# im2col on one core: the first load in two parts ahead of the barrier, single-plane copies, a first store in halves

## The chip, the core and the metric

The kernel runs on one of the cores of a Trainium2 chip. It uses three kinds of workers of that core: the DMA engines (16 of them), which move data between device memory (DRAM) and the core's on-chip memory; VectorE (DVE in the profile) and ScalarE (ACT), which copy inside the on-chip memory; and SyncE (SP), which issues the transfers. The on-chip memory has 128 partitions; a tile "128x900" has 900 numbers in each of them. TensorE (PE) and GpSimd (POOL) have no part in the computation.

The metric is the device time of one execution in microseconds (us).

## The reference

For an input of 16 images with 64 channels of 32x32 floats, `im2col` with a 3x3 kernel writes, for each image and channel, nine planes of 30x30: plane (ki, kj) is the channel's image, shifted by ki rows and kj columns.

```
for b in range(batch):
    for i in range(h_out):          # 30
        for j in range(w_out):      # 30
            patch = x[b, :, i:i+3, j:j+3]
            cols[b, :, i*w_out + j] = patch.ravel()
# cols: (16, 64*9, 900) float32
```

No arithmetic is done. 4.19 MB are read and 33.18 MB are written, nine planes of 900 for each channel of 1024.

## The kernel before

The 16x64 channels lie on 128 partitions, eight channels (`CPP`) on each. One input tile holds all eight channels, 32 KB per partition. It is loaded in two parts by SP: the first two channels (rows 0 to 64 of the 256 rows of 32 floats, 8 KB per partition) and the other six (24 KB per partition). Line 35 issues both.

The loop runs over four pairs of channels. For a pair there is an output tile of 2 x 9 x 900 floats (64.8 KB per partition); the pool has two buffers of it, so the third pair's copies wait until the first pair's store has landed. For each channel ScalarE copies the three planes of ki = 1 in one instruction (L55, 128x2700). VectorE copies the first two planes of ki = 0 and of ki = 2, two per instruction (L57, 128x1800). The planes that are left, (0,2) and (2,2), are one VectorE instruction for the first channel of a pair (L61), and one of VectorE (L65) and one of ScalarE (L68) for the second. Then SP stores the pair with one transfer of 64.8 KB per partition (L71), which in DRAM is contiguous for each partition.

The schedule is written by hand: each engine does its instructions in the order of the program, and waits at an instruction until the semaphores that it names have been reached. The order of transfers on SP's queue is the order in which they are issued. An instruction that must wait for several semaphores has the further ones in event instructions ahead of it. ScalarE's first copy brings a load of its function table (ACT_TABLE_LOAD, shown under L55), which is put directly ahead of that copy. After the program is compiled, the first load is taken out of its place and put at the very start, ahead of SP's drain, which begins the opening barrier of all engines; the rest of the work begins behind that barrier.

Of the kernel before, what the change touches and what calls it, by code (L numbers as in the profile page):

```python
# [1 line left out]

# [3 lines left out]


def _im2col(ctx, tc, x, K, out):


    nc = tc.nc
    P = nc.NUM_PARTITIONS

    B, C, H, W = x.shape
    HO = H - K + 1
    WO = W - K + 1
    KK = K * K
    assert out.shape == (B, C * KK, HO * WO)
    CPP = B * C // P
    assert CPP * P == B * C and C % CPP == 0 and CPP % 2 == 0 and K == 3  # L20

    x_v = x.rearrange("b (cp c2) h w -> (b cp) (c2 h w)", c2=CPP)
    out_v = out.rearrange("b (cp c2 kk) n -> (b cp) c2 (kk n)", c2=CPP, kk=KK)

    in_pool = ctx.enter_context(tc.tile_pool(name="in_pool", bufs=1))
    out_pool = ctx.enter_context(tc.tile_pool(name="out_pool", bufs=2))

    ctx.enter_context(tc.manual_schedule())

    in_tile = in_pool.tile([P, CPP, H, W], x.dtype, name="in_tile")  # L30
    in_flat = in_tile.rearrange("p c h w -> p (c h w)")

    def load(r0, r1):

        return nc.sync.dma_start(
            out=in_flat[:, r0 * W : r1 * W],
            in_=x_v[:, r0 * W : r1 * W],
        )

    first = load(0, 2 * H)  # L40
    load(2 * H, CPP * H)

    def planes(c, ki, kj, n, step):

        w = in_tile[:, c, ki : ki + HO, kj : kj + WO]
        part, row, col = [list(d) for d in w.ap]
        return bass.AP(w.tensor, w.offset, [part, [step, n], row, col])

    for c in range(0, CPP, 2):
        out_tile = out_pool.tile([P, 2, KK, HO, WO], x.dtype, name="out_tile")  # L50


        for s in range(2):
            o = out_tile[:, s]
            nc.scalar.copy(out=o[:, K : 2 * K], in_=planes(c + s, 1, 0, K, 1))  # L55
            for ki in (0, 2):
                nc.vector.tensor_copy(  # L57
                    out=o[:, ki * K : ki * K + 2], in_=planes(c + s, ki, 0, 2, 1)
                )
            if s == 0:  # L60
                nc.vector.tensor_copy(  # L61
                    out=o[:, 2:KK:6], in_=planes(c + s, 0, 2, 2, 2 * W)
                )
            else:
                nc.vector.tensor_copy(  # L65
                    out=o[:, 2], in_=in_tile[:, c + s, 0:HO, 2 : 2 + WO]
                )
                nc.scalar.copy(  # L68
                    out=o[:, 8], in_=in_tile[:, c + s, 2 : 2 + HO, 2 : 2 + WO]
                )  # L70
        nc.sync.dma_start(  # L71
            out=out_v[:, c : c + 2].rearrange("p c n -> p (c n)"),
            in_=out_tile.rearrange("p c kk i j -> p (c kk i j)"),
        )
    return first


def kernel(
    tc: tile.TileContext,
    x: bass.AP,  # L80
    kernel_size: bass.AP,
    out: bass.AP,
):
    with ExitStack() as ctx:
        first = _im2col(ctx, tc, x, int(kernel_size), out)


    tc.close()
    tc.compile()  # L89
    blocks = tc.nc.main_func.blocks  # L90
    load = first.ins
    home = next(b for b in blocks if any(i.name == load.name for i in b.instructions))
    home.instructions = [i for i in home.instructions if i.name != load.name]
    head = list(blocks[0].instructions)
    at = next(
        k
        for k, i in enumerate(head)
        if i.engine == load.engine and type(i).__name__ == "InstDrain"
    )
    head.insert(at, load)  # L100
    blocks[0].instructions = head


# [1 line left out]
_INS = ['x', 'kernel_size']  # L105
_OUTS = [((16, 576, 900), 'float32')]

_NUMBERS = {'kernel_size': 3}


# [26 lines left out]
```

## Time and profile before

| what | value |
|---|---|
| median of 3 runs | 91.33 us (91.1 to 91.39) |
| profiled execution | 91.39 us, of which 89.6 are the span |
| VectorE busy | 22.6 us, 24 instructions |
| ScalarE busy | 23.8 us, 13 instructions |
| DMA queue | 864 packets, 37.37 MB, 97.2% of 16 engines' span |
| copy on ScalarE, 128x2700 / 128x900 | 2443 / 938 ns |
| copy on VectorE, 128x1800 / 128x900 | 1092 / 620 ns |
| table load on ScalarE | 1283 ns, once |

The span goes from the first instruction of the program to the last; the time of a run has about 1.8 us more around it. In the profile "SPq" is SP issuing a transfer; a transfer's landing is when its semaphore is reached. A line of the timeline gives the start and the duration in us, the engine, the line of the kernel, the operation and the shape; in brackets stands how long the engine had been idle before, and what ended that. Instructions of one kind that follow one another are merged into one line ("x2"). Where two copies follow directly, the second starts a little before the first one's end.

### The profile page before, as it was taken

How to read it: one execution, taken by the hardware profiler on the slowest of the kernel's cores; microseconds unless marked ns; L12 is line 12 of the kernel's file. 1: busy time of each engine (PE TensorE's matmuls, PEld its weight loads, DVE VectorE, ACT ScalarE, POOL GpSimd, SP SyncE). 2: the span in 40 equal slices, each digit the busy share in tenths (PEclk: the TensorE clock that was granted, in tenths of full speed). 3: DMA queues.
4: the chain of work that ended last, by engine and by line, in shares of the span. 5: the costliest groups of instructions: out<-in, count | busy, mean ns of one | idle time of the engine just before them, and what ended most of it. 6: DMA issues, size and time to landing. Idle time of an engine off the chain costs nothing.

```text
span 89.6 us, 96 instructions
## 1 busy us (share of the span) xinstructions
DVE 22.6 (25%) x24; ACT 23.8 (27%) x13; POOL 0.2 (0%) x4
## 2 busy tenths in 40 slices
DVE  0079759900000099500000399100000000000000
ACT  5079759900000099500000399100000000000000
POOL 0000000000000000000000000000000000000000
DMA  5989899999999999947999999999999982999990
GB/s 128 505 384 494 362 463 463 463 463 463 463 463 463 463 463 463 434 174 318 463 463 463 463 463 463 463 463 463 463 463 463 463 347 116 463 463 463 463 463 0
DMA packets 864, 37.37 MB, mean 417 GB/s; under 512 B 96, under 2 KB 96, under 8 KB 96
## 3 DMA queue, kind: packets, MB, share of 16 engines
q1 hardware_dynamic: 864, 37.37, 97.2%
HBM read 4.19 MB, written 33.18 MB: 417 GB/s over the span
## 4 chain that ended last, share of the span: by engine, by line
DMA 49%; DVE 12%; DVEq 1%; issue 0%; SPq 0%
DMA out_dram<-out_tile 36%; DMA in_tile<-in_x_dram 13%; DVE out_tile L57 8%; DVE out_tile L61 2%; DVE out_tile L65 1%; DVEq L89 1%; DVEq L57 0%; SPq L71 0%
## 5 line engine op out<-in xcount | busy, mean ns | idle before, releaser
L55 ACT COPY out_tile<-in_tile 128x2700 f32<-128x2700 f32 x8 | 19.2, 2443 | 31.7 <-DMA out_dram<-out_tile 27.1
L57 DVE COPY out_tile<-in_tile 128x1800 f32<-128x1800 f32 x16 | 16.8, 1092 | 33.7 <-DMA out_dram<-out_tile 27.1
L61 DVE COPY out_tile<-in_tile 128x1800 f32<-128x1800 f32 x4 | 4.4, 1090 | 0.0
L68 ACT COPY out_tile<-in_tile 128x900 f32<-128x900 f32 x4 | 3.8, 938 | 0.0
L65 DVE COPY out_tile<-in_tile 128x900 f32<-128x900 f32 x4 | 2.5, 620 | 0.0
L55 ACT ACT_TABLE_LOAD x1 | 1.3, 1283 | 0.8 <-PEq L118 0.8
L118 POOL MEMSET const-bfloat16-1.0<- 128x1 bf16 x1 | 0.1, 101 | 0.0
L118 POOL MEMSET const-uint8-127<- 128x1 uint8 x1 | 0.1, 101 | 0.0
L118 POOL MEMSET const-float32-0.0<- 128x1 f32 x1 | 0.1, 98 | 0.2 <-issue 0.2
L118 POOL MEMSET const-float32-1.0<- 128x1 f32 x1 | 0.1, 98 | 0.0
## 6 DMA issues: line engine op xcount, KB each, us to landing
out_dram<-out_tile SPq DMA_DIRECT2D x4, 8100.0 KB, 32.4
in_tile<-in_x_dram SPq DMA_DIRECT2D x1, 3072.0 KB, 11.4
in_tile<-in_x_dram SPq DMA_DIRECT2D x1, 1024.0 KB, 4.9
```

The lines of the kernel that those rows point to most:

```text
L55: nc.scalar.copy(out=o[:, K : 2 * K], in_=planes(c + s, 1, 0, K, 1))
L57: nc.vector.tensor_copy(out=o[:, ki * K : ki * K + 2], in_=planes(c + s, ki, 0, 2, 1))
L61: nc.vector.tensor_copy(out=o[:, 2:KK:6], in_=planes(c + s, 0, 2, 2, 2 * W))
L65: nc.vector.tensor_copy(out=o[:, 2], in_=in_tile[:, c + s, 0:HO, 2 : 2 + WO])
L68: nc.scalar.copy(out=o[:, 8], in_=in_tile[:, c + s, 2 : 2 + HO, 2 : 2 + WO])
L89: tc.compile()
L118: nc = _bacc.Bacc("TRN2", target_bir_lowering=False, num_devices=1)
```

## The change

The first load is now two: rows 0 to 16 (2 KB per partition) and rows 16 to 64 (6 KB). Both are put at the very start, ahead of SP's drain. The third part, 24 KB, is issued where the second one was.

Each plane is a copy of its own (128x900), 72 in all. For channel 0, ScalarE takes the six planes with kj = 0 or 2 and VectorE the three with kj = 1. From then on a pattern of five gives two planes to ScalarE and three to VectorE. The first pair is stored in two transfers, one for each channel (32.4 KB per partition), each issued when its nine planes are there; the other three pairs are stored as before.

```diff
-    first = load(0, 2 * H)
-    load(2 * H, CPP * H)
+    cuts = [0, 16, 2 * H, CPP * H]
+    first = [load(nc.sync, r0, r1) for r0, r1 in zip(cuts[:2], cuts[1:3])]
+    load(nc.sync, cuts[2], cuts[3])
...
+    on_act = (False, True, False, True, False)
+    n = 0
     for c in range(0, CPP, 2):
         out_tile = out_pool.tile([P, 2, KK, HO, WO], x.dtype, name="out_tile")
         for s in range(2):
-            o = out_tile[:, s]
-            nc.scalar.copy(out=o[:, K : 2 * K], in_=planes(c + s, 1, 0, K, 1))
-            for ki in (0, 2):
-                nc.vector.tensor_copy(
-                    out=o[:, ki * K : ki * K + 2], in_=planes(c + s, ki, 0, 2, 1)
-                )
-            if s == 0:
-                nc.vector.tensor_copy(
-                    out=o[:, 2:KK:6], in_=planes(c + s, 0, 2, 2, 2 * W)
+            for kk in range(KK):
+                ki, kj = divmod(kk, K)
+                src = in_tile[:, c + s, ki : ki + HO, kj : kj + WO]
+                dst = out_tile[:, s, kk]
+                if kk % 3 != 1 if c + s == 0 else on_act[n % len(on_act)]:
+                    nc.scalar.copy(out=dst, in_=src)
+                else:
+                    nc.vector.tensor_copy(out=dst, in_=src)
+                n += 1
+            if c == 0:
+                nc.sync.dma_start(
+                    out=out_v[:, s],
+                    in_=out_tile[:, s].rearrange("p kk i j -> p (kk i j)"),
                 )
-            else:
-                nc.vector.tensor_copy(
-                    out=o[:, 2], in_=in_tile[:, c + s, 0:HO, 2 : 2 + WO]
-                )
-                nc.scalar.copy(
-                    out=o[:, 8], in_=in_tile[:, c + s, 2 : 2 + HO, 2 : 2 + WO]
-                )
-        nc.sync.dma_start(
-            out=out_v[:, c : c + 2].rearrange("p c n -> p (c n)"),
-            in_=out_tile.rearrange("p c kk i j -> p (c kk i j)"),
-        )
+        if c > 0:
+            nc.sync.dma_start(
+                out=out_v[:, c : c + 2].rearrange("p c n -> p (c n)"),
+                in_=out_tile.rearrange("p c kk i j -> p (c kk i j)"),
+            )
     return first
...
-    load = first.ins
...
+    for load in (f.ins for f in first):
...
+        head.insert(at, load)
+        blocks[0].instructions = head
```

More of the change, by code (lines that the diff above doesn't have):

```diff
@@ L19, in _im2col @@
     CPP = B * C // P
-    assert CPP * P == B * C and C % CPP == 0 and CPP % 2 == 0 and K == 3
+    assert CPP * P == B * C and C % CPP == 0 and CPP % 4 == 0
     x_v = x.rearrange("b (cp c2) h w -> (b cp) (c2 h w)", c2=CPP)
@@ L31, in _im2col, with load @@
     in_flat = in_tile.rearrange("p c h w -> p (c h w)")
[L33 to L37, printed above, removed]
-        )
-    first = load(0, 2 * H)
-    load(2 * H, CPP * H)
[L43 to L47, printed above, removed]
+    def load(queue, r0, r1):
+        return queue.dma_start(
+            out=in_flat[:, r0 * W : r1 * W], in_=x_v[:, r0 * W : r1 * W]
+        )
+    cuts = [0, 16, 2 * H, CPP * H]
[3 more added lines that the diff above has]
+    n = 0
     for c in range(0, CPP, 2):
@@ L90 @@
     blocks = tc.nc.main_func.blocks
-    load = first.ins
[L92 to L101, printed above, removed]
+    for load in (f.ins for f in first):
+        home = next(
+            b for b in blocks if any(i.name == load.name for i in b.instructions)
+        )
+        home.instructions = [i for i in home.instructions if i.name != load.name]
+        head = list(blocks[0].instructions)
+        at = next(
+            k
+            for k, i in enumerate(head)
+            if i.engine == load.engine and type(i).__name__ == "InstDrain"
+        )
+        head.insert(at, load)
+        blocks[0].instructions = head
 _INS = ['x', 'kernel_size']
```

## The prediction

> **What bounds the kernel now.** I read the page's summary and DMA rows first, then the timeline up to the first store, then the chain and the DMA queue's own waits. The page:
>
> ```profile
> span 89.6 us, 96 instructions
> ...
> DVE 22.6 (25%) x24; ACT 23.8 (27%) x13; POOL 0.2 (0%) x4
> ...
> DMA  5989899999999999947999999999999982999990
> ...
> q1 hardware_dynamic: 864, 37.37, 97.2%
> ```
>
> The copying engines work a quarter of the span; the 16 DMA engines work 97% of it. The dips (4, 7 and 8, 2) are no idleness: a packet is booked in the slice where it starts, and a store packet lasts about 2.4 us, longer than a slice of 2.24. In the trace's packet records each DMA engine runs from about 1.0-1.4 us to 88.2-88.3 us without a pause, but for one: between the loads and the first store. So only three things can move the time: bytes moved, packet overhead, and whether a DMA engine finds its queue empty. The timeline of the head shows where the queue can run empty:
>
> ```profile
> 0.00 1.12 SPq L35 DMA_DIRECT2D in_tile<-in_x_dram  x2
> ...
> 0.78 1.28 ACT L55 ACT_TABLE_LOAD   x1 [0.78 <-PEq L118]
> 4.93 4.79 ACT L55 COPY out_tile<-in_tile 128x2700 f32<-128x2700 f32 x2 [2.87 <-DMA in_tile<-in_x_dram]
> 4.93 2.10 DVE L57 COPY out_tile<-in_tile 128x1800 f32<-128x1800 f32 x2 [4.93 <-DMA in_tile<-in_x_dram]
> ...
> 9.63 0.94 ACT L68 COPY out_tile<-in_tile 128x900 f32<-128x900 f32 x1
> 9.97 0.62 DVE L65 COPY out_tile<-in_tile 128x900 f32<-128x900 f32 x1
> 10.69 0.35 SPq L71 DMA_DIRECT2D out_dram<-out_tile  x1
> ```
>
> The ACT table load runs at 0.78, under the first load, and is done 2.87 us before the data come: free. Both engines copy from 4.93 to 10.6, and the first store is issued at 10.69. By the packet records the loads run out on the 16 DMA engines between 11.26 and 11.83, and the first store packets start 0.85 to 0.99 us after the issue (11.54 to 11.68): twelve engines stand idle for 15 to 418 ns. Of the two engines that end last (both 88.33), one had waited 418 ns and one not at all. So the issue at 10.69 stands just at the edge: earlier gains next to nothing, and **every microsecond later is paid in full**. From there on the stores follow one another; first two pieces of the chain (start, length, what), then a row of SP's waits (total, times, longest):
>
> ```profile
> 17.95 32.59 DMA out_dram<-out_tile
> 50.53 0.03 issue
> ```
> ```profile
> SPq L89 <- DMA out_dram<-out_tile: 31.9, 2, 19.1
> ```
>
> The second store is issued at 17.95 and lands at 50.53, the first at 31.39 (10.69 plus its 20.7 to landing): 19.1 us apart, 8.29 MB at 433 GB/s. The last one ends the kernel, though the chain stops short of it.
>
> **The change, part by part.**
>
> *The load split.* Bytes are the same. An 8 KB packet takes 309 ns and a 24 KB packet 912 in the packet records, so a packet has a fixed (3x309-912)/2 = 7.5 ns; 8 more per engine cost 0.06 us. The first load now lands at 4.91; the 6 KB part will at 4.97. Its issue comes one issue later (382 ns); hidden if the 2 KB packets keep the engines busy that long. Eight take about 8x83 = 0.66 us, after a first packet that took 0.2 to 0.84 us over its 309, so I take it as hidden; ends 4.91 and 5.35. Nothing is computed on the 2 KB alone: every copy reads 30 rows of its channel, the part holds 16.
>
> *SP ahead of the barrier.* The second issue (0.33 to 0.38) delays SP's drain and so the barrier, now over at 0.72, by about 0.35 for all engines; POOL's memsets lie before it. The big load goes from 0.79 to about 1.15; its packets come some 1.0 to 1.4 us after the issue (as the first load's do) and are wanted at 4.0: 1.4 us of cover, and nothing is paid.
>
> *The table load moves behind a wait.* A copy must now wait for two loads. Built, ACT's order reads:
>
> ```
> 1 L55 LoadActFuncSet [waits DMAHW1_49]
> 2 L55 TensorCopy out_tile_67<-in_tile_63 128x900 [waits DMAHW0_49]
> 3 L55 TensorCopy out_tile_67<-in_tile_63 128x900 x8
> ```
>
> One wait stays on the copy; the other became an instruction of its own, and the table load stands after it. DMAHW1 is the 6 KB load. Everything of ACT queues behind it, so the table load leaves its cover (0.78 to 2.07) for the critical stretch. A wait of its own costs 0.10 us (store landed 31.39, ACT's copy at 31.49) against 0.02 of a direct one (4.91, 4.93). Table load from 5.07, for 1.28, to 6.35. What lies between it and the first copy no row shows, since the copy waited for data anyway: from -0.10 (two copies on ACT overlap: 2x2443 ns are 4.79 us) to 2.87 (the idle stretch that would have hidden it). I take 0, by the nearest row, copy behind copy.
>
> The Trainium skill ("ScalarE: Activation LUTs", What ACT_TABLE_LOAD costs) gives the load 1283 ns, as this trace does, and adds a drain of about 1380 ns, 2.66 us in all; no run here shows the drain. If it comes after the load, this sum would end 1.4 us higher, near 93.6 us as an estimate; if it runs alongside, nothing is added.
>
> *Channel 0's copies: ACT gets six planes, VectorE three.* At 938 ns each, less 95 of overlap, 843: 5x0.843+0.938 = 5.15 us. From 6.35 to 11.50. VectorE: 2x0.54+0.62 = 1.7, done near 6.8; it isn't the limit. Without the table load ACT would be done at 10.2.
>
> *First store, half as long.* Its wait on VectorE is long met, that on ACT direct: issue 0.05 after the last copy (between 0.02 and 0.10), 11.55 against 10.69: +0.86. First packets from 12.40 to 12.54; meanwhile all 16 engines have been empty since 11.3 to 11.9. Split in two, the store has 8 more packets per engine: at 7.5 ns, +0.06. Rows on both sides (24 KB and 64.8 KB packets, 26.9 and 27.1 bytes per ns) leave no room for more at 32.4 KB.
>
> The Trainium skill ("SBUF — State Buffer", The DMA setup-cost knee) speaks against splitting: about 2 us for every transfer. Here stores queued one behind another land 19.1 us apart, at their plain rate. By the rule two more transfers would make this 4 us slower; by the trace nothing beyond the packets.
>
> *The rest, under cover.* ACT's three planes of channel 1 end at 11.50+3x0.84 = 14.0, and the second half goes out while the first half's 9.6 us run to 22: 8 us of cover. The following pairs cost ACT 7 or 8 planes, at most 7x0.843+0.938 = 6.8 us against 5.7 now; the store of the third pair goes out 13.3 us before the one ahead of it lands (37.25, 50.53), so 1.1 more is free. Were that cover gone, it would cost 1.1 each time.
>
> **Sum:** 0.06 + 0.08 (wait of its own) + 1.28 (table) + 0 (behind it) + 5.15 of copies against 5.66 now (-0.51) - 0.05 (issue) = +0.86; +0.06 for the halves: +0.92. The profiled run took 91.39 (89.6 of span and 1.8 around it), 0.06 above the median of 91.33. From the median: **92.25 us**.
>
> **The rivals.**
> 1. *The table load stays free.* If the chip starts it at the barrier all the same, the copies run from 5.0 to 10.2, the store goes out 0.5 us earlier than now, and the pauses of 15 to 418 ns go. But the engine that never paused ends at 88.33 regardless, and the extra packets cost 0.12: about 91.4, no change. It decides as soon as ACT's first copy starts before 5.5. Against it: the instruction order, and that ACT's copies at 31.49 and 50.63 each begin behind such a wait. Chance 0.06; with luck in the first packets (their delays differ by 0.6 us) faster than by 0.3%, 0.02.
> 2. *There is more behind the table load.* Anything up to 2.87 us; the end follows one for one, to 95.1. For it: no row excludes it. Against: no other pair of ACT instructions has such a pause. Chance 0.10 for more than 0.7 us.
> 3. *The 6 KB part lands late,* by its whole issue: +0.38, 92.6. Against: the 2 KB part covers it. Chance 0.08.
>
> **How the numbers follow.** My forecast has 0.74, by itself 91.9 to 92.5. Below: -0.06 (no packet cost of the load), -0.10 (overlap), -0.06 (halves), and most of the spread of the runs (from the median of 91.33 down to 91.1): 91.85. Above: rival 3 whole, +0.05 at the issue, and up to 0.25 of something behind the table load: 92.95. Left out are rival 1 and the longer part of rival 2, under 0.2. Measured to 0.3% (0.27 us, about what can be told from no change), rivals 2, 3 and the forecast are slower: 0.92; 0.06 same, 0.02 faster.
>
> **What would show it.** Right: ACT's table load near 5.1 instead of 0.78, its wait put down to the load; six ACT copies from about 6.35 to 11.5; first store issued near 11.55; a pause of about 0.6 to 1.2 us on the DMA engines ahead of 12.5; afterwards stores gapless, ACT's waits for buffers still above 10 us. Wrong: a table load near 1.1 (rival 1), a gap between it and the first copy (rival 2), a landing of the 6 KB part after 5.2 (rival 3). I would also be wrong if 2 KB or 32.4 KB packets ran well below their neighbours' rate.

## The result and the profile after

The changed kernel takes 92.65 us (median of 6 runs, 92.21 to 93.01) against 91.25 (6 runs, 91.1 to 91.39): ratio 1.0155, 95% interval 1.0123 to 1.0186, so 1.4 us slower. The forecast was 92.25 with a range of 91.85 to 92.95. The direction and the range held. The working did not hold throughout: the term that the forecast was built on costs 0.6 to 0.7 us where 0.92 had been given, and another one, put at 0.06 us, adds 0.7 us to it. The range held by luck, as the section on why the prediction was right shows.

The profiled execution took 92.21 us, the quickest of the six. Its page, the lines that answer to those of before:

```profile
span 90.4 us, 140 instructions
...
DVE 22.4 (25%) x41; ACT 27.8 (31%) x32; POOL 0.2 (0%) x4
...
DMA  5989897999999939999999999999999639999990
...
q1 hardware_dynamic: 1152, 37.37, 96.6%
```

The bytes are the same, the packets more (1152 against 864, semaphore writes included), and the DMA engines are still busy for almost the whole span. The span is only 0.8 us longer. The head of the timeline:

```profile
0.00 1.59 SPq L35 DMA_DIRECT2D in_tile<-in_x_dram  x3
...
4.93 1.28 ACT L55 ACT_TABLE_LOAD   x1 [4.93 <-DMA in_tile<-in_x_dram]
4.96 4.93 DVE L57 COPY out_tile<-in_tile 128x900 f32<-128x900 f32 x9 [4.96 <-DMA in_tile<-in_x_dram]
6.23 13.61 ACT L55 COPY out_tile<-in_tile 128x900 f32<-128x900 f32 x16
11.42 2.87 SPq L60 DMA_DIRECT2D out_dram<-out_tile  x2
```

The table load has moved from 0.78 to 4.93 us, its idle time put down to the load, as foreseen. VectorE starts its copies at once; ScalarE starts at 6.23, 0.01 us behind the table load. The first store goes out at 11.42 instead of 10.69. The chain of the head now has the table load as a piece of its own (start, length, what):

```profile
0.43 4.43 DMA in_tile<-in_x_dram
...
4.93 1.28 ACT L55
6.22 0.01 issue
6.23 13.62 ACT out_tile L55 x16
19.85 0.02 issue
19.86 31.46 DMA out_dram<-out_tile
```

Later waits for buffers are as ample as before (total, times, longest):

```profile
DVE out_tile L57 <- DMA out_dram<-out_tile: 27.0, 2, 13.7
ACT out_tile L55 <- DMA out_dram<-out_tile: 24.7, 2, 12.5
```

So far all is as predicted. What was not is in the DMA packet records (each load is 128 packets, one for each partition, eight on each of the 16 engines). In the kernel before, all 128 packets of the 24 KB load took 912 ns and the loads ended on the 16 engines between 11.24 and 11.83 us. Now 13 of the 128 took over 5% more, up to 1212 ns, and there are pauses between load packets that the kernel before did not have (about 0.2 us for an engine on average). Fourteen engines end their loads by 11.87, two at 12.50 and 12.57. The page's row of the load says the same in its last number, first before, then after:

```profile
in_tile<-in_x_dram SPq DMA_DIRECT2D x1, 3072.0 KB, 11.4
```

```profile
in_tile<-in_x_dram SPq DMA_DIRECT2D x1, 3072.0 KB, 11.6
```

It was issued 0.47 us later and took 0.2 us longer, so it landed at 12.91 us against 12.19. The first store packets start at 12.26 to 12.42 on the fourteen engines, at 12.50 and 12.57 on the two, and the last store packet of the kernel ends at 89.14 us, 76.57 behind the later of these; in the kernel before the stores of an engine take 76.4 to 76.8 us. Two delays therefore end at nearly the same moment in this run, and the profile alone cannot say which of them costs the time.

### The profile page after: what moved, and what is told of

Read it like the earlier page. It is cut to its first block, busy times and chain, and to the rows that moved or that the text cites. A ratio compares the mean times of both kernels' runs of the same rounds, so it can differ in the third digit from the quotient of the medians.

```text
span 90.4 us, 140 instructions
## 1 busy us (share of the span) xinstructions
DVE 22.4 (25%) x41; ACT 27.8 (31%) x32; POOL 0.2 (0%) x4
## 2 busy tenths in 40 slices
DMA packets 1152, 37.37 MB, mean 413 GB/s; under 512 B 128, under 2 KB 128, under 8 KB 384
## 3 DMA queue, kind: packets, MB, share of 16 engines
q1 hardware_dynamic: 1152, 37.37, 96.6%
## 4 chain that ended last, share of the span: by engine, by line
DMA 40%; ACT 16%; DVE 6%; DVEq 1%; SPq 0%; issue 0%; ACTq 0%
DMA out_dram<-out_tile 35%; ACT out_tile L55 15%; DVE out_tile L57 6%; DMA in_tile<-in_x_dram 5%; ACT L55 1%; DVEq L83 1%; SPq L35 0%; DVEq L57 0%; ACTq L55 0%
## 5 line engine op out<-in xcount | busy, mean ns | idle before, releaser
L55 ACT COPY out_tile<-in_tile 128x900 f32<-128x900 f32 x31 | 26.5, 941 | 24.7 <-DMA out_dram<-out_tile 24.7
L57 DVE COPY out_tile<-in_tile 128x900 f32<-128x900 f32 x41 | 22.4, 622 | 35.0 <-DMA out_dram<-out_tile 27.0
```

Source lines behind the costliest of these rows:

```text
L55: nc.scalar.copy(out=dst, in_=src)
L57: nc.vector.tensor_copy(out=dst, in_=src)
```

## The experiments

The theories: **T**, the late table load delays the first store, and that is the loss. **L**, the split load is slow by itself, whenever the store is issued. Ratios are to the kernel before, with 95% intervals.

### The parts, one by one

**The table load early, all else as changed.**

```diff
+    warm_tile = in_pool.tile([P, 2], x.dtype, name="warm_tile")
+    nc.vector.memset(warm_tile[:, 0:1], 0.0)
+    nc.scalar.copy(out=warm_tile[:, 1:2], in_=warm_tile[:, 0:1])
```

> The changed kernel with one addition: a one-column ScalarE copy of a zeroed scratch tile ahead of everything, so that the function table is loaded right behind the barrier and not behind the wait for the 6 KB load. Theory T (the table load on the path delays the first store, and that is the loss): ScalarE's first plane starts at about 4.95, the first store is issued near 10.1, time 91.2 to 91.5 us, ratio to before 1.000 to 1.003. Theory L (the split load itself is slower: in the changed kernel's profile two DMA engines end their loads at 12.50 and 12.57 us, against 11.83 for the latest before, so the last store ends late whenever the first is issued): the first store is early all the same, but time stays at 92.0 to 92.6.

Measured: 92.25 us, 1.0114 (1.0091 to 1.0138). From the timeline:

```profile
1.25 1.28 ACT L47 ACT_TABLE_LOAD   x1 [1.25 <-PEq L118]
2.54 0.19 ACT L47 COPY warm_tile<-warm_tile 128x1 f32<-128x1 f32 x1
5.03 9.38 ACT L59 COPY out_tile<-in_tile 128x900 f32<-128x900 f32 x11 [2.29 <-DMA in_tile<-in_x_dram]
10.21 2.87 SPq L64 DMA_DIRECT2D out_dram<-out_tile  x2
```

The table load is free again and the store goes out 1.2 us earlier, and still 1 us of the loss stays. T as the whole of the loss is refuted. In the packet records the engines hardly wait for the store any more (17 ns on average); one ends its loads at 12.22.

**The first 8 KB as one load, all else as changed.**

```diff
-    cuts = [0, 16, 2 * H, CPP * H]
-    first = [load(nc.sync, r0, r1) for r0, r1 in zip(cuts[:2], cuts[1:3])]
-    load(nc.sync, cuts[2], cuts[3])
+    first = [load(nc.sync, 0, 2 * H)]
+    load(nc.sync, 2 * H, CPP * H)
```

> The changed kernel with the first 8 KB again as one load; single-plane copies, ScalarE's six planes of channel 0 and the two half stores stay. T and L alike: the copy waits for one load, so the table load is free, and the loads are those of before: first store near 10.1, loads end near 11.8, time 91.2 to 91.4, ratio 1.000 to 1.003. If the single-plane copies or the half stores cost something by themselves, it stays above 91.6.

Measured: 91.34 us, 1.0014 (1.0005 to 1.0024). First store at 10.03; one slow packet of 24 KB, loads ended by 11.73.

```profile
0.80 1.28 ACT L54 ACT_TABLE_LOAD   x1 [0.80 <-PEq L113]
4.84 9.38 ACT L54 COPY out_tile<-in_tile 128x900 f32<-128x900 f32 x11 [2.76 <-DMA in_tile<-in_x_dram]
10.03 2.87 SPq L59 DMA_DIRECT2D out_dram<-out_tile  x2
```

The split load brings all but 0.13 us of the loss, by one way or both; the 72 single-plane copies and the half stores cost these 0.13 us together (0.05 to 0.22 by the interval).

**The split alone, in the kernel before, table load early.** The three lines of the first experiment, and:

```diff
-    first = load(0, 2 * H)
+    first = [load(0, 16), load(16, 2 * H)]
```

both put ahead of the barrier as in the change.

> The kernel before with the first load in 2 and 6 KB, both ahead of the barrier, and the small ScalarE copy that loads the table early; copies and stores as before. Theory L (the split load is slow by itself): the same loss as in the changed kernel with the early table, 92.0 to 92.6, ratio 1.008 to 1.014, with some DMA engines ending their loads after 12.0. If the loss needs the single-plane copies or the half stores as well: 91.2 to 91.5.

Measured: 92.34 us, 1.0108 (1.0080 to 1.0137). The page's row of the load, and the timeline:

```profile
in_tile<-in_x_dram SPq DMA_DIRECT2D x1, 3072.0 KB, 11.9
```

```profile
0.00 1.59 SPq L35 DMA_DIRECT2D in_tile<-in_x_dram  x3
...
11.22 0.35 SPq L75 DMA_DIRECT2D out_dram<-out_tile  x1
```

L holds without any other part of the change: 20 of the 24 KB packets were slow (up to 1434 ns), three engines ended their loads at 12.34, 12.48 and 12.88, and the end follows the last of them. The 6 KB part landed at 5.37 here, 0.46 later than the 8 KB did, and so the store went out at 11.22 instead of 10.69. The other thirteen engines waited for it (first packets at 12.06 to 12.21) and ended by 88.85 us, against 88.33 in the kernel before; the last engine ended at 89.33. So in this profiled run, by estimate, the late landing alone would have cost about half of the microsecond, and the slow packets the rest. The early table load was not run by itself; but slow 24 KB packets show without it too, in the changed kernel (13) and in the run with channel 0 dealt the other way below (4 begun before 5 us), while the kernels with the first load whole have one such packet before 5 us at most.

**The late table load alone, in the kernel before.** VectorE first writes one column of the plane that ScalarE's first copy overwrites, so that this copy has two waits:

```diff
+            if c + s == 0:
+                nc.vector.tensor_copy(
+                    out=o[:, K, 0, 0:1], in_=in_tile[:, 0, 0, 0:1]
+                )
             nc.scalar.copy(out=o[:, K : 2 * K], in_=planes(c + s, 1, 0, K, 1))
```

> The kernel before, loads untouched, with one addition: VectorE first copies a single column into the plane that ScalarE's first copy overwrites, so that this copy has two things to wait for, and the table load stands behind the wait for the first load. T: table load at 5.0 to 6.3, ScalarE's copies to 12.0, first store issued near 12.05 instead of 10.69, and the end follows one for one: 91.25+1.36 = 92.6, ratio 1.015. L alone (a late table load costs nothing): 91.25, ratio 1.000.

Measured: 92.39 us, 1.0123 (1.0110 to 1.0136); four runs within 0.14 us.

```profile
4.83 1.28 ACT L59 ACT_TABLE_LOAD   x1 [4.83 <-DMA in_tile<-in_x_dram]
6.12 4.79 ACT L59 COPY out_tile<-in_tile 128x2700 f32<-128x2700 f32 x2
10.82 0.94 ACT L72 COPY out_tile<-in_tile 128x900 f32<-128x900 f32 x1
11.78 0.35 SPq L75 DMA_DIRECT2D out_dram<-out_tile  x1
```

The mechanism of T is real: with clean loads (ended by 11.68) all engines wait for the first store, whose packets start at 12.63 to 12.78.

**The late table load alone, in the changed kernel with one load.** The same single column, ahead of plane 0, on top of the one-load kernel.

> The changed kernel with the first 8 KB as one load (which alone brought 91.34) and a single-column VectorE copy into the plane that ScalarE's first copy overwrites: loads of before, but the table load behind the wait. It measures the prediction's sum by itself. T: table load 4.9 to 6.2, six copies to 11.4, first store issued near 11.45, first packets 12.3 to 12.5, all DMA engines idle before that: 91.34+0.75 to 0.9 = 92.1 to 92.25, ratio 1.009 to 1.011, little scatter. If the late table load costs nothing without the split load: 91.3.

Measured: 91.94 us, 1.0080 (1.0065 to 1.0095). The table load ran at 4.63, the store went out at 11.12, its packets started at 11.96 to 12.11, the loads had ended by 11.45. This is the forecast's sum with the load split left out of it: +0.71 us over the 91.23 of the kernel before, where 0.86 and 0.06 had been reckoned.

```profile
4.63 1.28 ACT L58 ACT_TABLE_LOAD   x1 [4.63 <-DMA in_tile<-in_x_dram]
11.12 2.88 SPq L63 DMA_DIRECT2D out_dram<-out_tile  x2
```

In the profiled run the 8 KB landed at 4.56, 0.35 earlier than in the run of before, and from landing to issue it is 6.56 us, as reckoned (11.55-4.97 = 6.58). The landing moves from run to run: in the seven profiled runs with the 8 KB whole it lies between 4.56 and 4.91. The prediction read it from the latest of them, which put the first store just at the edge; with an earlier landing there is some slack, and that fits the missing 0.2 us, though no run shows it by itself.

### What in the split slows the loads

**Three loads, but the first one whole:** the 24 KB in two loads of 12 KB.

```diff
-    load(2 * H, CPP * H)
+    load(2 * H, 5 * H)
+    load(5 * H, CPP * H)
```

> The kernel before with the first 8 KB as one load and the other 24 KB in two loads of 12 KB: also three loads, but none of 2 KB and only one ahead of the barrier. Theory N (one more load in the queue is what slows the loads): 92.0 to 92.6. Theory S (it is the small packets at the very start) and theory B (it is two loads issued back to back ahead of the barrier): 91.2 to 91.45, loads ending by 11.9.

Measured: 91.27 us, 1.0014 (1.0002 to 1.0025). N falls: a third load in the queue costs 0.1 us. The longest 12 KB packet took 509 ns, the median is 460; loads ended by 11.56 us.

**The 6 KB part behind the barrier** (2 and 6 KB, early table load, only the first ahead of the barrier).

```diff
-    first = [load(0, 16), load(16, 2 * H)]
+    first = [load(0, 16)]
+    load(16, 2 * H)
```

> The kernel before with 2 and 6 KB and the early table load, the 6 KB issued behind the barrier at about 0.8 us instead of 0.4. S: as with both ahead of the barrier, 92.0 to 92.6, or 0.1 to 0.4 more, as the 2 KB run out before the 6 KB come. B: 91.2 to 91.5.

Measured: 1.0129 (1.0051 to 1.0207), from the two quickest of its four runs (91.78 and 92.98 us); the four spread from 91.78 to 94.36, so no finer reading is made of it. None is as fast as B has it (91.2 to 91.5), which speaks against B.

**Other cuts:** 3 and 5 KB, and 6 and 2 KB, otherwise the split alone with its early table load.

```diff
-    first = [load(0, 16), load(16, 2 * H)]
+    first = [load(0, 24), load(24, 2 * H)]
```

```diff
-    first = [load(0, 16), load(16, 2 * H)]
+    first = [load(0, 48), load(48, 2 * H)]
```

> The kernel before with the early table load and the first 8 KB in 3 and 5 KB, both ahead of the barrier. If the loss of the split comes from packets as small as 2 KB, it shrinks to a half or less: under 91.8. If any split of the very first load costs it, it stays: 92.0 to 92.6.

> The same with 6 and 2 KB: the large part first. If small packets at the very start are the cause, 91.2 to 91.6; if it is that a second load starts while the first one's packets are still young, or simply the second load, 92.0 to 92.6.

Measured: 92.39 us, 1.0125 (1.0103 to 1.0147), and 92.94 us, 1.0183 (1.0155 to 1.0212). The rows of the 24 KB load, 3 and 5 KB first, then 6 and 2:

```profile
in_tile<-in_x_dram SPq DMA_DIRECT2D x1, 3072.0 KB, 11.7
```

```profile
in_tile<-in_x_dram SPq DMA_DIRECT2D x1, 3072.0 KB, 12.3
```

S falls too: the loss doesn't shrink with larger parts, nor with the large part first. In all these cuts 24 KB packets from 4.0 us on are slow, up to 2.1 and 2.3 us each, long after the small parts are through. In the run with 6 and 2 KB both copying engines began after the 6 KB (at 4.07), and the store went out at 9.83; the next section bears on that, so part of its 1.7 us may be another matter. Why a split of the first load slows later packets stays open.

### A store issued early

**Channel 0 dealt the other way,** six planes to VectorE and three to ScalarE, in the changed kernel. It was meant as a second test of T.

```diff
-                if kk % 3 != 1 if c + s == 0 else on_act[n % len(on_act)]:
+                if kk % 3 == 1 if c + s == 0 else on_act[n % len(on_act)]:
```

> The changed kernel with the planes of channel 0 dealt the other way: six to VectorE, three to ScalarE. The table load stays behind the wait, at about 4.93 to 6.22, but ScalarE then ends near 8.9 and VectorE near 8.3, so the first store is issued near 8.9, well ahead of the loads' end. T (the table load costs only through the first store's issue): 91.2 to 91.5, ratio 1.000 to 1.003. L: as with the table load taken away, 92.0 to 92.6. If the late table load costs in another way than by the store's issue, this stays above 92 where the run with the early table load doesn't.

Measured: 92.85 us, 1.0189 (1.0152 to 1.0226): not better than the changed kernel, with the first store at 9.12. Seventeen of its packets of 24 KB that began from 10.25 us on, 1.1 us behind the issue, took 0.1 to 0.5 us too long. That was a third effect; two runs were made for it.

**The same dealing with one load.**

> The changed kernel with the first 8 KB as one load, and channel 0 dealt with six planes to VectorE and three to ScalarE: first store issued near 8.3 instead of 10.03. With the split load that dealing gave 92.85 where the other gave 92.25, and 17 packets of 24 KB after 9.5 us took 0.1 to 0.5 us more than 912 ns. If a store queued early behind a running load slows the load: 91.7 to 92.2 and slow 24 KB packets from about 9.3 on. If the slow packets come from the split alone: 91.25 to 91.45 and none.

Measured: 92.61 us, 1.0155 (1.0140 to 1.0170), where the kernel with one load and the change's own dealing has 91.34.

```profile
8.07 3.55 SPq L59 DMA_DIRECT2D out_dram<-out_tile  x2
```

```profile
in_tile<-in_x_dram SPq DMA_DIRECT2D x1, 3072.0 KB, 12.5
```

Every packet of 24 KB begun up to 8.83 us was normal; all 32 that began from 9.40 on, 1.33 us behind the issue, were slow, up to 1736 ns.

**The kernel before with its first store in halves,** its copies untouched.

```diff
+            if c == 0:
+                nc.sync.dma_start(
+                    out=out_v[:, s], in_=o.rearrange("p kk i j -> p (kk i j)")
+                )
-        nc.sync.dma_start(
+        if c > 0:
+            nc.sync.dma_start(
```

> The kernel before with nothing changed but the first pair's store in two halves, so that the first half is issued near 8.1 instead of 10.69, while the 24 KB load still runs; the copies stay as dealt before. Theory Q (a store queued behind a running load slows that load): 24 KB packets begun from 9.3 on take more than 912 ns, loads end past 12.4, 92.2 to 92.7. If the run with six planes on VectorE was slow because of VectorE's copies: 91.2 to 91.4, no slow packets.

Measured: 92.83 us, 1.0173 (1.0147 to 1.0199).

```profile
7.82 2.88 SPq L72 DMA_DIRECT2D out_dram<-out_tile  x2
```

```profile
in_tile<-in_x_dram SPq DMA_DIRECT2D x1, 3072.0 KB, 12.8
```

Q holds, and VectorE's copies are not the reason. The load needs 12.8 us instead of 11.4 to land; from 8.4 us on, 0.6 behind the issue, 45 of its last 48 packets take 0.2 to 1.0 us more, and nothing of it is won back: each engine begins its stores when its loads end (12.69 to 13.34), and they run at their usual rate. Stores issued at 10.03, 10.21 and 10.69 did no such harm: the last 24 KB packets had begun at 10.81, 11.30 and 10.92 there, 0.8, 1.1 and 0.2 us behind the issue. That fits the 1.1 and 1.3 us of the two runs with the other dealing; the 0.6 of this run it does not explain. What in the engine slows the load is not shown by these runs.

No variant beat the kernel before. Those with one load for the first 8 KB and a first store at 10.0 to 10.4 come within 0.14%.

## Why the prediction was right, and where it wasn't

- **What bounds the kernel: right.** The end of every kernel follows the moment when the last DMA engine begins its stores, 76.4 to 76.9 us before its last packet.
- **The table load behind a wait: right,** almost to the number. Table load at 4.93 (5.07 predicted), first copy at 6.23 (6.35), sixth copy done at 11.40 (11.50), store at 11.42 (11.55). Nothing lies between the table load and the first copy: 0.01 us, so rival 2 is out. The drain of about 1380 ns that the Trainium skill ("ScalarE: Activation LUTs", What ACT_TABLE_LOAD costs) adds to a table load does not show behind this one, the only one of the kernel. With clean loads the late table load, together with the copies and the half stores, costs 0.7 us (predicted 0.9); the size was somewhat too large.
- **"The load split": wrong.** The step gave it 0.06 us, eight more packets per engine at 7.5 ns. The packets themselves take about what it reckoned: the median 2 KB packet 84 ns and the 6 KB packet 234, 9 ns more than the 309 of 8 KB. But it took for granted that packets of the load behind would go on taking 912 ns. Measured alone with an early table load, the split costs 1.0 us (ratio 1.0108, 1.0080 to 1.0137), in slow 24 KB packets, pauses, engines that end their loads unevenly and, in that run, a late landing of the 6 KB. The packets' plain rate, read from a trace where nothing disturbs them, was no bound from above for this.
- **The sum: near by luck.** With the changed kernel's copies and stores, all four combinations were run: first load whole and table early 91.34 us, late table alone 91.94, split alone 92.25, both 92.65. So the term that the forecast was built on costs 0.6 us (0.7 with the copies and half stores, where 0.92 had been given), and the split, put at 0.06, adds 0.7 on top of it. The range reached 0.7 us above the forecast for other things, a late landing of the 6 KB and time behind the table load, which the profiled run doesn't show; the unforeseen term fell into that room. Delays of this kind need not add: each engine starts its stores at the later of two moments, the end of its own loads and the store's arrival, and in the profiled run fourteen engines waited for the store and two were held by their loads. In the times, 0.6 and 0.9 gave 1.3; the 0.2 between is less than the noise (0.4 us by the four intervals), so that they fall short of adding is not shown.
- **Rival 1 was priced wrong.** With the table load free it gave 91.4; measured so, the kernel takes 92.25.
- **Rival 3: not in the profiled run** (the 6 KB landed at 4.86), though in the split alone it landed at 5.37, past the 5.2 that the prediction had named as its sign; in the other two profiled runs with this cut ahead of the barrier it landed at 4.94 and 5.10. Its size of 0.38 was of the right order for a landing; the slow 24 KB packets behind it were not thought of.
- **Under cover, right:** SP's longer way to the barrier (24 KB issued at 1.26 and wanted at 4.0), the half stores, the slower copies of the later pairs. With one load the half stores and the copies together cost 0.13 us (1.0014), where 0.06 had been given.

## What to carry to other kernels

Where the DMA engines are never idle, look in the built order of instructions at what stands between a wait and the work behind it: a wait of two things became an instruction of its own here, and the table load behind it came onto the path; a tiny copy that needs no load keeps it off. Before delays that end in the same wait are summed, ask which of them comes last on each DMA engine: it starts at the later of them. Don't split a first load, nor issue a store while a long load still runs, on the ground that the bytes stay the same: measure what it does to the packets of the transfer in flight.

## What had not been expected of the hardware

- A store queued at 7.82, 9.12 or 8.07 us, while the load still ran, slowed that load from 0.6, 1.1 and 1.3 us behind its issue: packets of 24 KB took up to 1920, 1448 and 1736 ns instead of 912. With the first load whole the kernel took 1.6 us (7.82) and 1.4 us (8.07) more. Stores queued from 10.03 us on did not slow it.
- Cutting the first 8 KB per partition in two (2+6, 3+5, 6+2) costs 1.0 to 1.7 us with the early table load in place (the 1.7 may hold an early store's harm too), while cutting the 24 KB behind it in two costs 0.1.
- The loss is uneven: in the early-table run fifteen engines ended their stores by 88.45 us and one at 89.04. The kernel waits for that one.
